# Summing a small matrix product on VectorE instead of TensorE, in one layer of a two-block transformer kernel

## The chip, the cores and the metric

The kernel runs on one core of a Trainium2 chip. Its time is the device time of one execution, in microseconds (us); before the change it is 1560.64 us, the median of three runs (1558.99 to 1562.67). The profile is one execution taken by the hardware profiler. TensorE is called PE in its rows (PEld is its weight load), VectorE is DVE, ScalarE is ACT, GpSimd is POOL, and SP is the queue that starts the transfers (DMAs).

## The reference, cut to what matters

The program is a transformer: a first block of two layers on 256 tokens `x` and 256 context tokens `ctx` with 1024 features, then a second block of two layers on `x` alone. All data is float32. Each of the first block's layers is modulated by vectors that depend on a conditioning vector `c`:

```python
s_lat, s_ctx = silu(c), silu(c_ctx)              # vectors of 1024
for i in range(2):
    mod   = s_lat @ w_mod[i] + b_mod[i]          # 1024 x 6144 weights; a vector of 6144
    mod_c = s_ctx @ w_mod[i] + b_mod[i]          # the same for the context tokens
    x, xc = _layer(x, xc, mod, mod_c, rope, i < 1, p)   # the last layer returns no context
# in _layer: six chunks of 1024 each
sh1, sc1, g1, sh2, sc2, g2 = split(mod, 6)       # csh1, csc1, ... from mod_c
h = rms_norm(x) * g_pre * (1 + sc1) + sh1        # hc from xc in the same way
...                                              # mixers on h and hc, x = x + g1 * norm(y)
h = rms_norm(x) * g_pre * (1 + sc2) + sh2        # the feed-forward part
x = x + g2 * norm(square(relu(h @ w_ff1)) @ w_ff2)
```

The second layer (i = 1) needs its context tokens only as keys, values and states, so of its `mod_c` only the chunks sh1 and sc1 are used.

## The kernel before

Tokens go in four tiles of 128 (x 0, x 1, ctx 0, ctx 1), features in K tiles of 128. Every large product is done by `mm3`: a float32 operand is split into a high part (rounded by ScalarE, line 226) and a low part (source minus high part, by VectorE, line 227), and three products high x high, high x low and low x high are summed in PSUM (line 212). Weights are fetched in transfers of 512 KB into the pool `raw` (five buffers of 128 x 1024) and split into the pools `wh` and `wl` (ten buffers of 128 x 512 each). A raw buffer is given back when both halves of it have been split.

The modulation of the second layer is computed inside the feed-forward part of the first layer, `ffn(0, ...)`. That has eight rounds (`r_` from 0 to 7). A round has a first half, in which w_ff1's block gives four outputs of 24 matmuls each (one per `ft`), and a second half, in which w_ff2's rows give eight outputs of 12 matmuls each. After each `ft` of the rounds 1 to 7 the code calls `step(1)`, 28 calls in all, which advances a generator: `mod_steps` (line 284). One step fetches one K tile of 2048 columns of w_mod in two transfers of 512 KB and issues four float32 matmuls with a stationary operand of 128 x 32 (two columns of it hold the vectors for x and ctx), one for each 32-partition band of one PSUM bank (`fl`, line 303). Eight steps make a unit; the ninth copies the bank (line 307), transposes it in four blocks (line 310) and adds the bias into `mods[1]` (line 314). Three units give the six chunks: 24 such steps with 96 matmuls.

In the first half ScalarE applies relu and square to each output (lines 902, 903), GpSimd squares it again in full precision (line 904) and VectorE subtracts to get the low part (line 905). In the second half VectorE adds each output to an accumulator (line 921).

The order on each engine is made by a scheduler: it takes instructions in the order of the program as their inputs and buffers come free in its own model of time. On the chip each engine then runs its list strictly in order. Buffers that matter here: `q` (eight of 128 x 512; four hold the gates of `ffn` until round 7), `fl` (one PSUM bank), and five PSUM banks `mm` and `sc` that the outputs use in turn.

Of the kernel before, what the change touches and what calls it, by code (L numbers as in the profile page):

```python
# [26 lines left out]
def constants():  # L27
# [4 lines left out]
    # positions of the 256 tokens ordered by (t mod 4, t // 4 mod 4, t // 16)  # L32
# [11 lines left out]
    # rope of the latent attention: 32 dims as four blocks of 8  # L44
# [7 lines left out]
    # rope of the second block: 64 dims as two halves  # L52
# [12 lines left out]
def body(ctx, tc, A, out):  # L65
# [49 lines left out]
    def AN():  # L115
        """A bank of either kind in turn."""
        turn[0] += 1
        return MM() if turn[0] % 3 == 1 else SC()
# [13 lines left out]
    def bc(ap, n):  # L132
        """[128, h] as [128, h, n]."""
        return ap[:, :, None].to_broadcast([ap.shape[0], ap.shape[1], n])

    def sooner(offset):
        """Scheduled ahead of the order of the program by an offset, later for a negative one."""
# [7 lines left out]
    def steps_sooner(offset):  # L145
        """The same for the steps of a generator."""
# [13 lines left out]
    # ---- pieces  # L160
# [3 lines left out]
    def rpow(out, a, b, eps):  # L164
        """(a + b + eps) ** -0.5"""
# [4 lines left out]
    def wblk(src, segs, k0=0, nk=KT, keep=0, tag="u"):  # L170
        """Weight rows of nk K tiles, columns `segs`, as pairs of high and low parts by K tile."""
# [35 lines left out]
    def mm3(ps, pairs):  # L207
        """Sum over the pairs of stationary^T @ moving, each as a high and a low part."""
# [9 lines left out]
    def tok(hT, t, W):  # L218
        """Pairs for token tile t against the weights of one block."""
        return [(cut(hT[k], t * P, (t + 1) * P), W[k]) for k in range(len(W))]  # L220
# [8 lines left out]
    def silu2(o, src):  # L229
        """2 silu(src) = src * (1 + tanh(src / 2))"""  # L230
# [7 lines left out]
    # ---- what every phase uses  # L238
# [8 lines left out]
    def load_cols(i, eng):  # L247
        """Vectors of layer i, feature on partition: [128, 110]."""
# [15 lines left out]
    # residual streams, token-major, as two halves of the features: ctx 0, ctx 1, x 0, x 1  # L264
# [8 lines left out]
    # ---- modulation  # L273
# [10 lines left out]
    def mod_steps(i, segs, w, ps):  # L284
        """Modulation of layer i: four segments of w columns, given by their starts; feature on partition."""
# [33 lines left out]

    def mod_units(*units):  # L320
        """A step function for the given (layer, pair of chunks) pairs, to be called between other work."""
# [3 lines left out]
        it = steps()  # L325
# [8 lines left out]
    def mod_scale(i, chunk, o_g, ks=(0, 8), a=None):  # L334
        """gain * (1 + scale)"""
# [7 lines left out]
    def mod_gate(i, chunk, o_g, r):  # L343
        """gate * gain of the norm after it, the same row on all partitions."""
# [14 lines left out]
    def normed(tiles):  # L359
        """RMS norm of token tiles, without a gain."""  # L360
# [12 lines left out]
    def modulated(xn, kind, scale, shift, dst, ks=range(KT), o=0):  # L373
        """Modulation and transposition of normed token tiles into the pairs dst[k] from column o on, [feature, token]."""
# [11 lines left out]
    def postnorm(t, halves, gate):  # L386
        """x[t] += gate * rms_norm(y)."""
# [8 lines left out]
    def softmax(ps, n):  # L396
        """Softmax of the rows of [128, n]."""
# [7 lines left out]
    def softmax_masked(ps, mask):  # L405
        """Softmax of the rows of mask - scores, given the scores with the sign turned; the mask is 0 or far above."""
# [7 lines left out]
    def transposed(p, nb, tag):  # L414
        """The nb blocks of p, each transposed, side by side in SBUF."""
# [7 lines left out]
    def interleaved(parts, order):  # L423
        """Interleaves generators by their letters, then ends each of them."""
# [6 lines left out]
    # ---- first block  # L431
    X, CTX = (2, 3), (0, 1)

    def both():
        """Pairs by K tile for ctx and x side by side, and their two parts."""
# [3 lines left out]
    def mix(i, hT, W1, step):  # L439
        """Both mixers of layer i up to w_out: the pairs of the concatenated outputs, [feature, token]."""  # L440
# [28 lines left out]
        # latent attention and dt: columns of one block  # L469
        # K tiles 0 to 3 of the concatenated outputs by feature, 4 to 7 by token tile  # L470
# [9 lines left out]
        def to_y(src, k, t, n, eng=None):  # L480
            """Columns of n tokens from tile t on, into pair k."""
# [22 lines left out]
        def latents():  # L504
            for t in X + CTX:
# [27 lines left out]
                # the two latents, transposed  # L533
# [5 lines left out]
                # keys and values  # L539
# [12 lines left out]
                # queries  # L552
# [25 lines left out]
        def attention():  # L578
            """CTX queries see the ctx keys, x queries all."""
# [744 lines left out]
```

## Time and profile before

| | |
|---|---|
| time of a run, median of 3 | 1560.64 us (1558.99 to 1562.67) |
| span of the profiled execution, first to last instruction | 1557.8 us |
| TensorE busy | 1490.3 us, 96% |
| VectorE busy | 951.7 us, 61% |
| ScalarE busy | 737.4 us, 47% |
| GpSimd busy | 298.2 us, 19% |
| TensorE's granted clock, mean | 0.985 |

The profile gives the span of its execution, and no separate time for it; the median of the runs is 2.84 us above this span. A busy share is an average over the whole span. What bounds one stage is read from the busy time of the engines in that stretch and from the waits before their instructions.

### The profile page before, as it was taken

How to read it: one execution, taken by the hardware profiler on the slowest of the kernel's cores; microseconds unless marked ns; L12 is line 12 of the kernel's file. 1: busy time of each engine (PE TensorE's matmuls, PEld its weight loads, DVE VectorE, ACT ScalarE, POOL GpSimd, SP SyncE). 2: the span in 40 equal slices, each digit the busy share in tenths (PEclk: the TensorE clock that was granted, in tenths of full speed). 3: DMA queues.
4: the chain of work that ended last, by engine and by line, in shares of the span. 5: the costliest groups of instructions: out<-in, count | busy, mean ns of one | idle time of the engine just before them, and what ended most of it. 6: DMA issues, size and time to landing. Idle time of an engine off the chain costs nothing.

```text
span 1557.8 us, 23537 instructions
## 1 busy us (share of the span) xinstructions
PE 1490.3 (96%) x8573; PEld 1217.5 (78%) x8573; DVE 951.7 (61%) x1919; ACT 737.4 (47%) x1589; POOL 298.2 (19%) x354
## 2 busy tenths in 40 slices
PE   6988999999999999997989899999999999999998
PEld 4756678887777777777977689997888888878886
DVE  3668555562444333457796765666785786567866
ACT  3433445553233322336555655555466457535653
POOL 1235201240000110024141201112310220021110
PEclk9998999999999999998999999999999999999999
DMA  9754623324555535534314555565535551545442
GB/s 301 251 199 151 197 95 102 97 67 129 173 172 176 188 105 180 185 94 121 98 61 130 163 160 179 168 227 163 167 118 163 163 188 35 199 153 169 144 149 68
DMA packets 123431, 235.47 MB, mean 151 GB/s; under 512 B 11536, under 2 KB 29139, under 8 KB 123315
## 3 DMA queue, kind: packets, MB, share of 16 engines
q1 hardware_dynamic: 122432, 232.42, 46.1%
q0 software_dynamic: 704, 1.50, 0.3%
q8 instruction: 67, 1.10, 0.3%
q14 instruction: 49, 0.40, 0.1%
q10 hardware_dynamic: 179, 0.06, 0.0%
HBM read 232.82 MB, written 1.11 MB: 150 GB/s over the span
## 4 chain that ended last, share of the span: by engine, by line
PE 83%; DVE 7%; DMA 5%; issue 2%; ACT 1%; POOL 1%; SPq 0%; ACTq 0%; DVEq 0%; POOLq 0%
PE sc L212 47%; PE mm L212 21%; PE fl L303 3%; PE tp L418 3%; DVE wl L227 2%; DMA raw<-in_w_mod_dram 1%; DMA raw<-in_ple_w_gate_dram 1%; DVE u L737 1%; PE mm L594 1%; PE sc L1038 1%; PE fl L212 1%; PE sc L748 1%; PE sc L1063 1%; PE sc L589 1%; PE tp L379 1%
## 5 line engine op out<-in xcount | busy, mean ns | idle before, releaser
L227 DVE TENSOR_TENSOR wl<-raw,wh 128x512 fp32r<-128x512 f32 (+1 forms) x602 | 418.1, 730 | 209.4 <-ACT wh L226 206.3
L226 ACT CAST wh<-raw 128x512 fp32r<-128x512 f32 (+1 forms) x602 | 355.8, 620 | 312.3 <-PE sc L212 74.1
L212 PE MATMUL sc<-wh,u 128*128 128x512 f32 (+2 forms) x1416 | 458.4, 391 | 2.2 <-ACT u L226 1.9
L212 PEld LDWEIGHTS sc<-wh,u 128*128 128x128 f32 x1416 | 264.8, 189 | 59.1 <-ACT wh L226 4.5
L212 PE MATMUL sc<-wl,u 128*128 128x512 f32 (+2 forms) x708 | 273.6, 388 | 0.1
L212 PE MATMUL sc<-u,wh 128*128 128x256 f32 (+1 forms) x1072 | 266.7, 337 | 1.6 <-ACT wh L226 1.0
L212 PE MATMUL mm<-wh,u 128*128 128x512 f32 (+1 forms) x648 | 218.9, 395 | 1.0 <-ACT u L226 1.0
L212 PEld LDWEIGHTS sc<-u,wh 128*128 128x128 f32 x1072 | 183.6, 191 | 31.3 <-issue 9.6
L212 PE MATMUL sc<-u,wl 128*128 128x256 f32 (+1 forms) x536 | 178.6, 335 | 0.0
L212 PEld LDWEIGHTS sc<-wl,u 128*128 128x128 f32 x708 | 134.2, 190 | 24.8 <-DVE wl L227 0.5
L904 POOL TENSOR_TENSOR r<-r 128x256 f32<-128x256 f32 (+1 forms) x60 | 57.7, 963 | 447.4 <-ACT r L902 404.2
L212 PEld LDWEIGHTS mm<-wh,u 128*128 128x128 f32 x648 | 122.0, 189 | 26.2 <-ACT u L226 1.7
L212 PE MATMUL mm<-wl,u 128*128 128x512 f32 (+1 forms) x324 | 126.7, 391 | 0.0
L212 PE MATMUL mm<-u,wh 128*128 128x256 f32 (+1 forms) x512 | 117.6, 317 | 0.1
L212 PEld LDWEIGHTS sc<-u,wl 128*128 128x128 f32 x536 | 102.1, 191 | 9.7
L905 DVE TENSOR_TENSOR u<-r,u 128x256 fp32r<-128x256 f32 (+1 forms) x60 | 33.7, 562 | 112.8 <-POOL r L904 110.2
L212 PEld LDWEIGHTS mm<-u,wh 128*128 128x128 f32 x512 | 85.8, 191 | 10.3 <-issue 4.2
L212 PE MATMUL mm<-u,wl 128*128 128x256 f32 (+1 forms) x256 | 80.7, 315 | 0.0
L971 POOL TENSOR_TENSOR r<-r,r 128x512 f32<-128x512 f32 (+1 forms) x30 | 44.7, 1493 | 151.1 <-DVE r L969 151.0
L212 PEld LDWEIGHTS mm<-wl,u 128*128 128x128 f32 x324 | 61.5, 190 | 11.9
L303 PE MATMUL fl<-raw,c_sT 128*32 128x512 f32 (+1 forms) x576 | 65.2, 475 | 4.5 <-DMA raw<-in_w_mod_dram 2.9
L902 ACT ACTIVATE r<-sc 128x256 f32<-128x256 f32 (+1 forms) x42 | 20.5, 489 | 97.1 <-PE sc L212 97.0
(308 smaller groups left out, 1947.5 us busy)
## 6 DMA issues: line engine op xcount, KB each, us to landing
raw<-in_w_ff_dram SPq DMA_DIRECT2D x128, 512.0 KB, 4.9
raw<-in_w_mod_dram SPq DMA_DIRECT2D x80, 512.0 KB, 4.5
raw<-in_a_w_in_dram SPq DMA_DIRECT2D x80, 512.0 KB, 3.7
raw<-in_w_in_dram SPq DMA_DIRECT2D x32, 512.0 KB, 3.9
raw<-in_b_w_in_dram SPq DMA_DIRECT2D x18, 512.0 KB, 4.8
raw<-in_w_mod_dram SPq DMA_DIRECT2D x32, 256.0 KB, 5.0
raw<-in_w_out_dram SPq DMA_DIRECT2D x16, 512.0 KB, 3.8
raw<-in_ple_w_gate_dram SPq DMA_DIRECT2D x16, 512.0 KB, 4.3
```

The costliest lines, as they stand in the source:

```text
L212: PE.matmul(ps, s, m, start=(i == 0), stop=(i == n - 1))
L226: ACT.copy(h, src)
L227: (eng or DVE).tensor_tensor(l, src, f(h), ALU.subtract)
L303: PE.matmul(ps[32 * g:32 * g + 32, :], sT[:, k + q, :], rs[g // per][:, q, w * (g % per):w * (g % per) + w], start=(k + q == 0), stop=(k + ...
L379: PE.transpose(tp[:, q * P:(q + 1) * P], xn[q][k // 4][:, (k % 4) * P:(k % 4 + 1) * P], ident)
L418: PE.transpose(tp[:, b * P:(b + 1) * P], p[:, b * P:(b + 1) * P], ident)
L589: PE.matmul(ps[:, b * P:(b + 1) * P], qT[t][:, hs], kT[b][:, hs], start=True, stop=True, skip_group_check=True)
L594: PE.matmul(po[64 * e:64 * e + 64, hp * P:(hp + 1) * P], V[b // 2][:, 256 * (b % 2) + 64 * h:256 * (b % 2) + 64 * h + 64], pT[e][:, b * P: ...
L902: ACT.activation(r[:, a:b], ps[:, a:b], AF.Relu)
L904: POOL.tensor_tensor(f2[:, a:b], r[:, a:b], r[:, a:b], ALU.mult)
L905: DVE.tensor_tensor(l, f2[:, a:b], f(h), ALU.subtract)
L971: POOL.tensor_tensor(a[:, 0:w], a[:, 0:w], b[:, 0:w], ALU.add)
```

## The change

The second layer's modulation is done by a new generator `mod_sums`. VectorE multiplies each half of a fetched tile (128 x 512 of one K tile) by the vector's entries, one scalar per partition, and adds the product to an accumulator of 128 x 512 in the pool `q`. After all eight K tiles the accumulator holds, per partition, the sum over row tiles; TensorE then sums over the partitions by a matmul with a stationary operand of ones (128 x 32). Four accumulators make one group: both vectors for the column blocks 0, 1, then both for 2, 3, then the vector for x alone for the blocks 4 to 7 and 8 to 11 (so the context vector is computed for the first two chunks only). Each transfer now holds two K tiles of 512 columns; there are 48 transfers of 512 KB, as before. `step(2)` is called in place of `step(1)`; the generator has 52 steps and there are 28 calls. The file also loses its comments and docstrings. Line numbers below the new code grow by 41 (905 becomes 946, 921 becomes 962).

```diff
+    ones = C([P, 32], "c_ones")
+    POOL.memset(ones, 1.0)
+
+    def mod_sums(i):
+        nrow = A["w_mod"][i].rearrange("(k p) n -> p k n", p=P)
+        for kinds, nb, b0 in (((0, 1), 2, 0), ((0, 1), 2, 2), ((0,), 4, 4), ((0,), 4, 8)):
+            accs = []
+            for b in range(b0, b0 + nb):
+                acc = [Q() for _ in kinds]
+                accs += acc
+                for k in range(0, KT, 2):
+                    r = raw.tile([P, 1024], F32, tag="raw", name=nm("raw")).rearrange("p (k c) -> p k c", k=2)
+                    SP.dma_start(r, nrow[:, k:k + 2, 512 * b:512 * b + 512])
+                    for q in range(2):
+                        for o, a in zip(kinds, acc):
+                            w = sT[:, k + q, o:o + 1]
+                            if k + q == 0:
+                                DVE.tensor_scalar(a, r[:, q, :], w, None, ALU.mult)
+                            else:
+                                DVE.scalar_tensor_tensor(a, r[:, q, :], w, a, ALU.mult, ALU.add)
+                    yield
+            ps = FL()
+            for g, a in enumerate(accs):
+                PE.matmul(ps[32 * g:32 * g + 32, :], ones, a, start=True, stop=True, skip_group_check=True)
+            r = R()
+            ACT.copy(r, ps)
+            for j in range(4):
+                PE.transpose(ps[:, j * P:(j + 1) * P], r[:, j * P:(j + 1) * P], ident)
+            ...
+            for b in range(nb):
+                k = 4 * (b0 + b)
+                DVE.tensor_tensor(mods[i][:, k:k + 4, 0:nr], t4[:, b, :, :, 0],
+                                  cols[i][:, O_BM + k:O_BM + k + 4, None].to_broadcast([P, 4, nr]), ALU.add)
+            yield
...
-                        step(1)
+                        step(2)
...
-    step = mod_units((1, 0), (1, 1), (1, 2))
+    POOL.memset(mods[1], 0.0)
+    step = stepping(mod_sums(1))
```

The scheduler moves instructions. On TensorE, after the first output of round 2 (24 matmuls; `wh`, `wl` are the weight's parts, `u` the activations', `fl` the modulation's bank) there stood before:

```order
L212 MATMUL sc989_4066<-u620_2608,wh979_4054 128x512
L212 MATMUL sc989_4066<-u621_2609,wh979_4054 128x512
L212 MATMUL sc989_4066<-u620_2608,wl980_4055 128x512
L303 MATMUL fl915_3740<-raw992_4097,c_sT8_114 32x512 x2
L303 MATMUL fl915_3740<-raw993_4099,c_sT8_114 32x512 x2
L212 MATMUL sc994_4105<-u606_2594,wh962_4020 128x512
```

At the same place there now stand the four matmuls that close the first group (`q` are accumulators):

```order
L212 MATMUL sc993_4088<-u621_2610,wh983_4076 128x512
L212 MATMUL sc993_4088<-u622_2611,wh983_4076 128x512
L212 MATMUL sc993_4088<-u621_2610,wl984_4077 128x512
L346 MATMUL fl996_4119<-q916_3743,c_ones13_124 32x512
L346 MATMUL fl996_4119<-q917_3744,c_ones13_124 32x512
L346 MATMUL fl996_4119<-q928_3831,c_ones13_124 32x512
L346 MATMUL fl996_4119<-q929_3832,c_ones13_124 32x512
L212 MATMUL sc1001_4140<-u607_2596,wh966_4042 128x512
```

They stand once in a group and not once in a K tile, so in the round there is no such insertion after the other three outputs. The second group's are not together: in the second half of round 2 TensorE's list has one of them alone.

```order
L212 MATMUL mm1042_4367<-wh1031_4297,u988_4083 128x512
L212 MATMUL mm1042_4367<-wh1034_4303,u989_4084 128x512
L346 MATMUL fl1078_4508<-q999_4133,c_ones13_124 32x512
L212 MATMUL mm1042_4367<-wl1035_4304,u989_4084 128x512
L212 MATMUL mm1042_4367<-wh1034_4303,u990_4085 128x512
```

In all they stand at seven places: four together, then one, one and two, then four together, then one and three. On VectorE, from the last accumulation of round 1 into round 2, there stood before the four low parts of round 2's outputs (line 905) and the weight's low parts (line 227) for its second half:

```order
L921 TENSOR_TENSOR u883_3659<-u883_3659,mm960_4004 128x512
L905 TENSOR_TENSOR u982_4059<-r991_4092,u981_4058 128x512
L905 TENSOR_TENSOR u984_4061<-r996_4131,u983_4060 128x512
L227 TENSOR_TENSOR wl1011_4225<-raw1009_4222,wh1010_4224 128x512
L227 TENSOR_TENSOR wl1013_4229<-raw1009_4222,wh1012_4228 128x512
L905 TENSOR_TENSOR u986_4063<-r1001_4170,u985_4062 128x512
```

Now the second group's products (lines 340 and 342) come first; the piece shows the first of them.

```order
L962 TENSOR_TENSOR u884_3662<-u884_3662,mm964_4026 128x512
L340 TENSOR_SCALAR q998_4132<-raw1000_4134,c_sT8_114 128x512
L340 TENSOR_SCALAR q999_4133<-raw1000_4134,c_sT8_114 128x512
L340 TENSOR_SCALAR q1010_4220<-raw1012_4222,c_sT8_114 128x512
L340 TENSOR_SCALAR q1011_4221<-raw1012_4222,c_sT8_114 128x512
L342 SCALAR_TENSOR_TENSOR q998_4132<-raw1000_4134,c_sT8_114,q998_4132 128x512
L342 SCALAR_TENSOR_TENSOR q999_4133<-raw1000_4134,c_sT8_114,q999_4133 128x512
L946 TENSOR_TENSOR u986_4081<-r995_4114,u985_4080 128x512
L342 SCALAR_TENSOR_TENSOR q1010_4220<-raw1012_4222,c_sT8_114,q1010_4220 128x512
```

Between the last accumulation of round 1 and the first low part of the weights for round 2's second half there are now 4 TENSOR_SCALAR and 18 SCALAR_TENSOR_TENSOR products; q998 takes the buffer of a first-group accumulator, which is free when the four matmuls above have run. Behind `ffn(0)` the lists of all engines are the same but for some swaps of neighbours.

## Rows read from the trace of the kernel before

**Rows 1.** The page: span, busy times, slices of TensorE and its clock.
```profile
span 1557.8 us, 23537 instructions
PE 1490.3 (96%) x8573; PEld 1217.5 (78%) x8573; DVE 951.7 (61%) x1919; ACT 737.4 (47%) x1589; POOL 298.2 (19%) x354
```

**Rows 2.** Windows of 40 us in ffn(0): busy by engine, clock, DMA share, GB/s.
```profile
400.00:440.00 40.00, 40.00 (x189) 29.37 (x188) 12.90 (x20) 10.21 (x18) 3.32 (x4) 1.00 0.45 144
...
sum 320.00, PE 319.95 PEld 243.18 DVE 122.94 ACT 97.10 POOL 29.50; mean PE 39.99 PEld 30.40 DVE 15.37 ACT 12.14 POOL 3.69
```

**Rows 3.** The tile fl from 300 to 690 us: count, duration min/median/max, forms.
```profile
L303 PE MATMUL fl<-raw,c_sT x192: 592/593/617, 368.7 to 664.4; 128*32 128x512 f32 x192
...
L314 DVE TENSOR_TENSOR c_mod<-fl,c_cols x6: 158/165/177, 472.6 to 677.9; 128x16 f32<-128x16 f32 x6
```

**Rows 4.** TensorE's timeline (start us, duration us): start of round 1; one step; one transposition.
```profile
363.20 0.39 PE L212 MATMUL sc<-u,wh 128*128 128x512 f32 x1
...
416.39 0.62 PE L212 MATMUL sc<-u,wh 128*128 128x512 f32 x2
416.84 0.39 PE L212 MATMUL sc<-u,wl 128*128 128x512 f32 x1
417.16 1.06 PE L303 MATMUL fl<-raw,c_sT 128*32 128x512 f32 x8
418.16 0.73 PE L212 MATMUL sc<-u,wh 128*128 128x512 f32 x2
...
471.62 0.39 PE L212 MATMUL mm<-u,wh 128*128 128x512 f32 x1
471.85 0.60 PE L310 MATMUL fl<-c_ident,r 128*128 128x128 f32 x4
472.20 0.48 PE L212 MATMUL mm<-u,wh 128*128 128x512 f32 x1
```

**Rows 5.** VectorE's groups from 360 to 690 us: count, busy us, mean ns.
```profile
L227 DVE TENSOR_TENSOR wl<-raw,wh 128x512 fp32r<-128x512 f32 (+1 forms) x108 | 73.6, 714 | 82.4 <-ACT wh L226 82.2
L921 DVE TENSOR_TENSOR u<-u,sc 128x512 f32<-128x512 f32 x33 | 22.6, 686 | 32.4 <-PE sc L212 32.1
L905 DVE TENSOR_TENSOR u<-r,u 128x512 fp32r<-128x512 f32 x28 | 19.3, 688 | 81.7 <-POOL r L904 81.7
```

**Rows 6.** VectorE, two lines of the whole program: duration min/median/max in ns.
```profile
L394 DVE SCALAR_TENSOR_TENSOR x<-r,s,x x16: 739/748/948, 293.0 to 1072.8; 128x512 f32<-128x512 f32 x16
L394 DVE SCALAR_TENSOR_TENSOR u<-r,s,u x8: 739/744/1210, 316.2 to 719.9; 128x512 f32<-128x512 f32 x8
...
L369 DVE TENSOR_SCALAR q<-x,s x16: 479/484/491, 7.5 to 888.6; 128x512 f32<-128x512 f32 x16
```

**Rows 7.** VectorE by shape, whole program: one more group with two tensors.
```profile
L1220 DVE SCALAR_TENSOR_TENSOR r<-r,u 128x512 f32<-128x512 f32 x8 | 5.4, 689 | 7.4 <-ACT r L1219 7.3
```

**Rows 8.** Timelines of VectorE and SP at the end of round 0.
```profile
345.63 0.42 DVE L905 TENSOR_TENSOR u<-r,u 128x256 fp32r<-128x256 f32 x1 [0.51 <-POOL r L904]
...
343.95 32.87 SPq L297 DMA_DIRECT2D raw<-in_w_mod_dram  x8
```

**Rows 9.** Transfers of w_mod: from issue to landing.
```profile
DMA to landing us min/median/max: 3.6/4.7/7.7
```

**Rows 10.** SP's waits from 360 to 690 us: total us, times, longest.
```profile
SPq L297 <- DVE wl L227: 97.6, 30, 8.6
SPq L297 <- PE fl L303: 71.3, 10, 17.7
```

**Rows 11.** All engines around 391 us, and line 904 from 360 to 690 us.
```profile
390.54 1.30 DVE L227 TENSOR_TENSOR wl<-raw,wh 128x512 fp32r<-128x512 f32 x2 [0.65 <-ACT wh L226]
...
391.65 1.08 POOL L904 TENSOR_TENSOR r<-r 128x512 f32<-128x512 f32 x1 [6.89 <-ACT r L902]
392.06 1.82 DVE L227 TENSOR_TENSOR wl<-raw,wh 128x512 fp32r<-128x512 f32 x2 [0.23 <-ACT wh L226]
...
L904 POOL TENSOR_TENSOR r<-r x28: 1039/1040/1132, 369.6 to 676.9; 128x512 f32<-128x512 f32 x28
```

More of the change, by code (lines that the diff above doesn't have):

```diff
@@ L318, in mod_steps @@
         yield
+    ones = C([P, 32], "c_ones")
[25 more added lines that the diff above has]
+                PE.transpose(ps[:, j * P:(j + 1) * P], r[:, j * P:(j + 1) * P], ident)
+            nr = len(kinds)
+            t4 = ps.rearrange("p (j b r q) -> p b j r q", j=4, b=nb, r=nr)
+            for b in range(nb):
[3 more added lines that the diff above has]
+            yield
     def mod_units(*units):
@@ L324, in steps, with stepping @@
                 yield from mod_steps(i, [2048 * u + 512 * g for g in range(4)], 512, FL())
-        it = steps()
+        return stepping(steps())
+    def stepping(it):
         def step(n=1):
```

## The prediction

> **What bounds the kernel now.** I read the page first, then the windows of the stretch that the change touches, then the tile of the modulation's bank, then timelines of single places. The page shows TensorE busy for 96% of a span of 1557.8 us, VectorE for 61% [rows 1]. The windows from 360 to 680 us, rounds 1 to 7 of `ffn(0)`, are what counts: TensorE is busy for 319.95 of 320 us at a granted clock of 1.00 in each window, VectorE for 122.94 us [rows 2]. Time taken from TensorE there is time saved, as long as VectorE, which has some 197 us free there on average, delivers its parts in time. The tile of the bank gives what can be taken: 192 passes of line 303 (each of the 96 matmuls is two passes), all inside these rounds [rows 3].
>
> **TensorE, what goes.** An undisturbed matmul follows the one before it by 0.226 us: two in the 0.45 us from 416.39 to 416.84. Across one step of the modulation it is 418.16 - 416.84 = 1.32 us [rows 4]. A step costs 1.32 - 0.23 = 1.09 us, and 24 of them 26.2 us.
>
> **TensorE, what comes.** Sixteen summing matmuls have the form of the old ones (128 x 32 stationary, 512 columns). Four together I take at the price of a step, 1.09 us. The order has them at seven places, some alone; no row shows one alone. Two passes cannot cost more than eight, so 1.09 us a place is the upper end, 7.6 us for seven; the lower end is 16/96 of the old cost, 4.4 us. I take 7.6, since entering and leaving the narrow form is visible beside the passes (0.32 us from 416.84 to 417.16 instead of 0.23). The fourth group adds one set of four transposes: 472.20 - 471.62 - 0.23 = 0.35 us [rows 4]. TensorE thus loses 26.2 - 7.6 - 0.35 = 18.2 us of work; with the lower end 21.5.
>
> The Trainium skill bears on the lone ones: its page "TensorEngine Tiling (Array Packing)", section Tiling Modes, says that a change of the tiling mode drains TensorE. By that rule every place would pay the drain whatever it holds, which is the upper end, the value taken.
>
> **VectorE, what comes.** 128 products of 128 x 512: 16 that start an accumulator and 112 that add to one. For the first kind there is a row, 484 ns; for the second the nearest is line 394, also two tensors and a scalar per partition, 748 ns [rows 6]. The ends are 689 ns, from a row whose scalar is a constant [rows 7], and 1210 ns, the longest of line 394 [rows 6]. I take 748, the median of the same form: 16 x 0.484 + 112 x 0.748 = 91.5 us. The bias additions become twelve instead of six, 1 us more at 165 ns [rows 3]. Averaged over the rounds this fits. It isn't spread evenly: the first two groups take 64 products, for which rounds 1 and 2 have about 44 us each. VectorE's old work in a round is 16 low parts of weights, 8 accumulations and 4 low parts of outputs at about 0.69 us [rows 5], 19 us; 32 products add 4 x 0.484 + 28 x 0.748 = 22.9. That is 42 of 44 us, so in these two rounds the order within the queue decides.
>
> Round 1. The products can start once the first transfer has landed: issued at 343.95 [rows 8], 4.7 us to land [rows 9], so 348.7; VectorE's last task of round 0 ends at 346.05 [rows 8]. In the new order 18 products of 748 ns, 4 of 484 ns and 6 low parts of weights stand up to the last low part for the round's first output: 19.5 us, until 368.2. TensorE starts the round at 363.20 [rows 4] and needs this part after 29 matmuls, at 369.8. It fits with 1.6 us to spare. I put 1 us for waits here.
>
> Round 2. The second group needs the accumulators of the first, which are free once the four summing matmuls behind the round's first output have run, 24 x 0.226 + 1.09 = 6.5 us into the round. Then 4 + 18 products, two low parts of outputs, two bias additions and the first low part of a weight: 1.9 + 13.5 + 1.4 + 0.3 + 0.7 = 17.8, ready at 24.3 us. TensorE wants it after 96 matmuls, one place, one set of transposes and three more matmuls, at 23.9 us: 0.4 us late. Behind it products and low parts alternate at the pace at which they are wanted. Near the round's end the low parts for round 3 wait in VectorE's queue for their transfers, whose raw buffers come free only when the products are done (up to now TensorE freed them), and the accumulations of line 962, which free the PSUM banks, stand behind: by the same reckoning about 2 us.
>
> GpSimd adds to this. Where line 904 ran for 1.08 us at 391.65, the pair of low parts beside it took 1.82 us instead of 1.30 [rows 11]: 0.5 us lost for one. Up to three fall into the busy stretch of round 2: 1.6 us. Waits in round 2 come to 4 us.
>
> Rounds 3 to 7. With 16 products of 11 to 12 us a round VectorE is at 31 of 44 us. Its waits for an accumulator's buffer fall in the first half of a round, ahead of work that is wanted in the second. I put nothing; the cover is VectorE's 12 us of free time a round.
>
> **Transfers.** 48 of 512 KB before and after. SP has waited 97.6 us for low parts and 71.3 us for line 303 to free a raw buffer [rows 10]; the second kind now waits for VectorE. DMA is busy for 0.45 of the time in the window shown [rows 2], so I see no new bound there. The two memsets are GpSimd's, which is busy for 19% [rows 1].
>
> **Sum.** -18.2 + 1 + 4 = -13.2 us, a span of 1544.6. The profile gives no time of its own execution beyond its span; the median of the runs is 2.84 us above it. Keeping that, 1547.4, so **1547.5 us**, 0.8% faster. A difference below 0.2% (3.1 us) can't be told from none.
>
> **Rivals.**
>
> *GpSimd and VectorE shut each other out.* The row at 391.65 shows half a microsecond lost for one line 904. If each of them stops a full VectorE queue for its whole 1.04 us [rows 11], rounds 1 and 2 lose 8 x 1.04 = 8.3 us beside the 2.4 us of round 2: 18.2 - 10.7 = 7.5 us gained, 1553.1 us. Against it: VectorE lost half of 1.04, and round 1 has 1.6 us to spare. Chance 0.12. The Trainium skill, page "SBUF — State Buffer", section SBUF: two separate sides, has the rule: a VectorE operation with two SBUF inputs and a GpSimd operation that reads SBUF hold the shared port pair exclusively, for a whole instruction. The trace agrees with a loss and not with its full length.
>
> *VectorE becomes the bound in rounds 1 and 2, no change.* With products at 0.98 us, halfway to 1.21, the 56 adding products of these rounds take 13 us more, all of it behind a queue that is already full: -13.2 + 13 = 0, about 1560.5 us. For it: 42 of 44 us. Against it: in both groups of line 394 the median lies within 9 ns of the minimum, so 1210 was an exception. Chance 0.11. At 1.21 us each it would be 26 us and 1573, which I leave outside.
>
> *The raw buffers starve the weights, slower.* Five buffers serve products and weights. A tile whose four products take 3 us is held longer than by a 1.09 us step, and a weight's transfer is issued behind it. Every round has two weight blocks, 14 in all. If the last transfer of each comes late by half a landing, 2.35 us, TensorE loses 33 us against 18.2: 14.7 us slower, 1575 us. The point from which it decides is 18.2 / 14 = 1.3 us a block. For it: the 71.3 us SP already waits for line 303. Against it: in five of the seven rounds a tile has only two products of 1.5 us in all, and DMA is under half busy. Chance 0.09.
>
> That the change doesn't do what it says, leaving products for the end, I exclude: 28 calls of two steps cover 52 steps.
>
> **How the numbers follow.** The forecast with waits between 0 and 10 us, 1542 to 1552: 0.62. More than 18.2 us, since lone matmuls are cheaper: 0.06. Then 0.12, 0.11 and 0.09 as above. Faster: 0.62 + 0.06 + 0.12 = 0.80; same 0.11; slower 0.09. The range of 1541 to 1559 leaves out some 0.03 below, three quarters of the case without change and the slower one, 0.2 in all.
>
> **What would show it.** Line 303 has no passes behind 360 us; lines 346 and 350 take about 8 and 2 us. Rounds 3 to 7 get shorter by 3 to 4 us each, round 2 hardly. VectorE is busy some 92 us more. In round 2 TensorE waits for wl of line 227 and for line 962, about 4 us; if it waits more than 10 us there, or waits for wh and transfers in rounds 3 to 7, I am wrong. Line 342 far from 748 ns makes the second rival right. Behind 700 us nothing changes but the start.

## The result, and the profile after

The changed kernel takes 1545.02 us, the median of four runs (1543.72 to 1545.77), beside 1561.14 us (1558.99 to 1562.67) for the kernel before, which has a fourth run by now: ratio 0.9895, 95% interval 0.9883 to 0.9907. Run once more, in a series of its own, it took 1542.54 us (1538.66 to 1545.70) beside 1559.97: 0.9882, interval 0.9862 to 0.9901. It is faster, by 16.1 and 17.4 us; forecast were 1547.5 us and 13 us. Single runs of one kernel scatter, and the longer ones mostly show a lower granted clock: of the six runs of that series the shortest, 1538.66 us, had 0.988 and the longest, 1545.70 us, 0.981.

The page, as in [rows 1]: TensorE has lost 16 us of work, VectorE has gained 85.

```profile
span 1544.0 us, 23412 instructions
...
PE 1474.4 (95%) x8417; PEld 1216.4 (79%) x8417; DVE 1036.5 (67%) x2053; ACT 740.0 (48%) x1590; POOL 307.3 (20%) x356
```

The windows of [rows 2] (busy us of PE, PEld, DVE, ACT, POOL, with instruction counts; clock; DMA share; GB/s). TensorE is no longer quite full, from 440 to 480 us above all; VectorE goes from 122.94 to 213.37 us.

```profile
400.00:440.00 40.00, 39.87 (x181) 31.76 (x180) 28.73 (x44) 10.38 (x18) 5.66 (x4) 1.00 0.39 118
440.00:480.00 40.00, 39.04 (x166) 29.21 (x165) 29.59 (x49) 11.81 (x21) 3.87 (x3) 1.00 0.70 224
480.00:520.00 40.00, 40.00 (x178) 33.13 (x177) 27.55 (x44) 12.12 (x21) 3.72 (x3) 1.00 0.65 210
...
sum 320.00, PE 318.90 PEld 256.92 DVE 213.37 ACT 106.84 POOL 43.34; mean PE 39.86 PEld 32.11 DVE 26.67 ACT 13.36 POOL 5.42
```

The tile of the bank, as in [rows 3]: 32 passes in place of 192. The last row tells who waited for the bank: twice the first product of a group (line 340) could not start before the sums of the group ahead had freed its accumulator, 9.6 us of VectorE's time in all.

```profile
L346 PE MATMUL fl<-q,c_ones x32: 592/605/617, 416.0 to 649.9; 128*32 128x512 f32 x32
...
L350 PE MATMUL fl<-c_ident,r x16: 270/272/276, 422.3 to 657.0; 128*128 128x128 f32 x16
...
  DVE q L340: 9.6, 2
```

Where the time went is read from the first matmul of each round (start, duration). The kernel before, profiled a second time (the starts of rounds 1, 2 and 7):

```profile
364.71 0.61 PE L212 MATMUL sc<-u,wh 128*128 128x512 f32 x2
...
413.14 0.62 PE L212 MATMUL sc<-u,wh 128*128 128x512 f32 x2
...
653.35 0.62 PE L212 MATMUL sc<-u,wh 128*128 128x512 f32 x2
```

The changed kernel, rounds 1 to 7:

```profile
366.92 0.62 PE L212 MATMUL sc<-u,wh 128*128 128x512 f32 x2
...
410.44 0.62 PE L212 MATMUL sc<-u,wh 128*128 128x512 f32 x2
...
459.75 0.62 PE L212 MATMUL sc<-u,wh 128*128 128x512 f32 x2
...
504.95 0.39 PE L212 MATMUL sc<-u,wh 128*128 128x512 f32 x1
...
548.47 0.61 PE L212 MATMUL sc<-u,wh 128*128 128x512 f32 x2
...
594.91 0.62 PE L212 MATMUL sc<-u,wh 128*128 128x512 f32 x2
...
638.43 0.62 PE L212 MATMUL sc<-u,wh 128*128 128x512 f32 x2
```

Rounds 1 to 6, from the first row to the last, take 288.64 us before (288.57 in the first profile) and 271.51 after: 17.1 us less, which is the result. One by one the rounds after take 43.52, 49.31, 45.20, 43.52, 46.44 and 43.52; before, a round with four steps takes 48.43. Rounds 1, 4 and 6 have no matmul of the modulation any more, so **43.52 us is the bare round**. That gives the price of each place at which matmuls of the modulation stand, from whole rounds:

- a step, eight passes in one place: (48.43 - 43.52) / 4 = 1.23 us;
- round 3 has one place of passes and one set of transposes: 45.20 - 43.52 = 1.68, so a set of four transposes costs 0.45 us;
- round 5 has in addition a place with two passes alone: 46.44 - 45.20 = 1.24 us;
- round 2 has three places and one set, 3 x 1.23 + 0.45 = 4.14, but is 5.79 us above the bare round: 1.65 us are waits;
- before the change, rounds 3 and 5 took 47.51 and 47.35 us. Each had a step, a set, and one place where two steps stood side by side, so these sixteen passes cost 2.31 and 2.15 us.

The first of these two places, in TensorE's timeline of the kernel before:

```profile
477.18 1.93 PE L303 MATMUL fl<-raw,c_sT 128*32 128x512 f32 x16
```

Sixteen passes are busy for 1.93 us, eight for 1.06 and two for 1.05 (rows below), though each pass takes 0.6 us. So the matmuls of the four bands run beside each other, and a place costs the same only up to one matmul for each band; a second one behind it costs about 1 us more.

In the experiments below, places and sets in rounds 1 to 6 are counted in the timeline, and "rest" is what remains of the six rounds above 6 x 43.52 + 1.23 a place + 0.45 a set: waits of TensorE. (Before the change the 22 are steps, at 20 places. The rest is below zero there, since a pair of steps side by side is a little cheaper than two apart.)

| kernel | rounds 1 to 6, us | places, sets | rest, us | median of runs, us | ratio to before (95%) |
|---|---|---|---|---|---|
| before | 288.57 | 22, 2 | -0.5 | 1561.14 | |
| changed | 271.51 | 6, 3 | 1.7 | 1545.02 | 0.9895 (0.9883, 0.9907) |
| the same again | 271.52 | 6, 3 | 1.7 | 1542.54 | 0.9882 (0.9862, 0.9901) |
| products thin | 266.25 | 3, 3 | 0.1 | 1541.33 | 0.9877 (0.9862, 0.9892) |
| products twice | 282.10 | 10, 3 | 7.3 | 1552.03 | 0.9951 (0.9934, 0.9968) |
| both vectors for all | 277.09 | 9, 5 | 2.7 | 1550.05 | 0.9939 (0.9922, 0.9955) |
| two chunks on TensorE | 274.33 | 10, 2 | 0.0 | 1545.38 | 0.9913 (0.9898, 0.9928) |
| sums together | 267.87 | 3, 3 | 1.7 | 1540.42 | 0.9867 (0.9842, 0.9891) |
| products spread | 268.73 | 5, 3 | 0.1 | 1543.11 | 0.9882 (0.9861, 0.9904) |
| no square on GpSimd | 270.25 | 6, 3 | 0.4 | 1545.07 | 0.9889 (0.9864, 0.9913) |
| together and spread | 267.34 | 3, 3 | 1.2 | 1540.18 | 0.9867 (0.9844, 0.9890) |
| the same again | 268.38 | 3, 3 | 2.2 | 1542.37 | 0.9881 (0.9858, 0.9904) |
| sums apart | 281.52 | 14, 3 | 1.8 | 1552.40 | 0.9966 (0.9951, 0.9981) |

The median less the six rounds lies between 1269.9 and 1275.1 us in every row: the rounds explain the times, to some 2.5 us of scatter. All but three kernels have a single profile, and the rest is not the same in each execution: the two profiles of "together and spread" have 1.2 and 2.2 us of it.

### The profile page after: what moved, and what is told of

The parts are those of the page before. It is cut to its first block, busy times and chain, and to the rows that moved or that the text cites. A ratio compares the mean times of both kernels' runs of the same rounds, so it can differ in the third digit from the quotient of the medians.

```text
span 1544.0 us, 23412 instructions
## 1 busy us (share of the span) xinstructions
PE 1474.4 (95%) x8417; PEld 1216.4 (79%) x8417; DVE 1036.5 (67%) x2053; ACT 740.0 (48%) x1590; POOL 307.3 (20%) x356
## 4 chain that ended last, share of the span: by engine, by line
PE 81%; DVE 9%; DMA 5%; issue 2%; ACT 2%; POOL 1%; SPq 0%; ACTq 0%; DVEq 0%; POOLq 0%
PE sc L212 46%; PE mm L212 19%; PE tp L459 3%; DVE wl L227 2%; PE fl L303 2%; DMA raw<-in_w_mod_dram 2%; DMA raw<-in_ple_w_gate_dram 1%; DVE u L778 1%; PE mm L635 1%; PE sc L1079 1%; PE fl L212 1%; PE sc L789 1%; PE sc L630 1%; DMA raw<-in_w_in_dram 1%; PE sc L1104 1%
## 5 line engine op out<-in xcount | busy, mean ns | idle before, releaser
L945 POOL TENSOR_TENSOR r<-r 128x256 f32<-128x256 f32 (+1 forms) x60 | 64.1, 1069 | 421.6 <-ACT r L943 374.7
L342 DVE SCALAR_TENSOR_TENSOR q<-raw,c_sT,q 128x512 f32<-128x512 f32 x112 | 84.9, 788 | 14.1 <-DMA raw<-in_w_mod_dram 13.5
L227 POOL TENSOR_TENSOR u<-r,u 128x256 fp32r<-128x256 f32 (+1 forms) x48 | 38.9, 817 | 122.8 <-ACT u L226 122.6
```

The costliest lines, as they stand in the source:

```text
L227: (eng or DVE).tensor_tensor(l, src, f(h), ALU.subtract)
L342: DVE.scalar_tensor_tensor(a, r[:, q, :], w, a, ALU.mult, ALU.add)
L945: POOL.tensor_tensor(f2[:, a:b], r[:, a:b], r[:, a:b], ALU.mult)
```

## The experiments

The theory: in these rounds TensorE has next to no other waits, and the time is a bare round plus a fixed price for each place at which the narrow form (128 x 32) interrupts the large matmuls, with two passes as with eight. The rivals: VectorE, whose work has grown, sets part of the time; or the price goes by passes.

**Is VectorE's added work in the way? Thin products.** The products that add read and write 16 of 512 columns, so the modulation is left incomplete.

```diff
-                                DVE.scalar_tensor_tensor(a, r[:, q, :], w, a, ALU.mult, ALU.add)
+                                DVE.scalar_tensor_tensor(a[:, 0:16], r[:, q, 0:16], w, a[:, 0:16], ALU.mult, ALU.add)
```

> Each of the 112 adding products works on 16 columns instead of 512, so the modulation is not complete; transfers, buffers and summing matmuls stay, and the order now has the sums at four places instead of seven. My theory (the change is paid and earned in TensorE's own list, and VectorE's load costs TensorE only the 2 us of waiting in round 2): three places of 1.05 us and 2.2 us of waiting go, 5.4 us less than the changed kernel's 1545.0, so 1539.6. Rival (VectorE's load slows TensorE in every round, so that the gain could have been much larger): 8 us less or more, below 1537. Rival (TensorE waits for the raw buffers' transfers, not for VectorE): as the changed kernel but for the three places, 1542.

Measured 1541.33 us. A product took 238 ns in the mean instead of 788, some 62 us less for VectorE, and the six rounds lost 5.26 us. Of these, three places fewer make 3.7 us (each group's four sums now stand together), and the waits make 1.6. By its time alone the kernel stands nearer to the 1542 us of the rival with the raw buffers than to the theory's 1539.6. The rounds decide: by that rival only the three places would have gone, and the waits of round 2 are gone too. So VectorE's work costs next to nothing as such; it costs places and the waits of round 2.

**Products twice.** Each adding product is issued a second time, so the sums are other ones.

```diff
                                 DVE.scalar_tensor_tensor(a, r[:, q, :], w, a, ALU.mult, ALU.add)
+                                DVE.scalar_tensor_tensor(a, r[:, q, :], w, a, ALU.mult, ALU.add)
```

> Every adding product is issued twice, so the modulation's values change; VectorE has 112 x 0.75 = 84 us more. My theory (VectorE is hidden only as long as a round's work fits beside TensorE's 44 us): rounds 1 and 2 have 63 us of VectorE's work, of which some 17 us can be done in round 0, rounds 3 to 7 have 42 us; the time grows by 20 to 35 us to 1565 to 1580, nearly all of it in rounds 1 and 2. Rival (the raw buffers are what is short): every round grows by more than 3 us. Rival (VectorE has room enough everywhere): under 1550.

Measured 1552.03 us: this expectation was wrong, by far for the theory and by 2 us for the rival of room enough. VectorE is now all but full in the windows from 400 to 480 us, and 278.80 us busy in all:

```profile
400.00:440.00 40.00, 37.43 (x155) 27.26 (x154) 39.81 (x63) 8.94 (x15) 5.60 (x4) 0.99 0.40 127
440.00:480.00 40.00, 39.89 (x162) 30.31 (x161) 38.93 (x62) 9.22 (x16) 1.50 (x2) 0.97 0.60 184
...
sum 320.00, PE 316.21 PEld 249.22 DVE 278.80 ACT 100.15 POOL 44.64; mean PE 39.53 PEld 31.15 DVE 34.85 ACT 12.52 POOL 5.58
```

Yet 112 more products, 87.7 us of work, cost 10.6 us in the rounds: 5 are places (ten instead of six, since sums that come later fall apart) and 5.6 waits, with a dip of the granted clock to 0.97 within them. The longest wait is for a high part of a weight; another is for a low part (in brackets the idle time before the matmul and what ended it):

```profile
436.85 0.50 PE L212 MATMUL sc<-wh,u 128*128 128x512 f32 x1 [1.45 <-ACT wh L226]
...
439.01 0.50 PE L212 MATMUL sc<-wl,u 128*128 128x512 f32 x1 [0.65 <-DVE wl L227]
```

I had held the products of a group to the rounds in which the kernel calls them. They are not held there: of the 120 products of the first two groups 18 ran in round 0, 42 and 51 in rounds 1 and 2, and 9 in round 3. VectorE took them up in rounds that it filled almost to the end: 44.32 of 46.20 us in round 1 and 52.69 of 52.87 us in round 2.

**The price of a place: sums apart.** Each accumulator is summed as soon as it is complete, so that the same 16 matmuls stand at 15 places.

```diff
-            accs = []
+            ps, todo, g = FL(), [], 0
...
+                    if k == KT - 2:
+                        todo += acc
+                    if todo:
+                        PE.matmul(ps[32 * g:32 * g + 32, :], ones, todo.pop(0), start=True, stop=True, skip_group_check=True)
+                        g += 1
                     yield
...
-            for g, a in enumerate(accs):
+            for a in todo:
...
```

> Each accumulator is summed over its partitions as soon as it is complete, not when its group is: the same 16 summing matmuls now stand at 15 places, 14 of them in rounds 1 to 6, where the changed kernel has 6. Theory (a place costs about 1.2 us, whatever it holds): rounds 1 to 6 take 6 x 43.54 + 14 x 1.2 + 3 x 0.48 = 279.5 us without waits, 8 us more than the 271.5 of the changed kernel, 1553 us. Rival (the price goes by passes, 1.22 / 8 = 0.15 us each): 30 passes cost 4.6 us wherever they stand, rounds 1 to 6 take 267 us and as much as now beside the waits, 1541 to 1545 us.

Measured 1552.40 us, and 281.52 us for the six rounds. The rows are the start of round 1, a lone place, the only marked wait of the six rounds, and the start of round 7:

```profile
364.45 0.62 PE L212 MATMUL sc<-u,wh 128*128 128x512 f32 x2
...
375.42 1.04 PE L345 MATMUL fl<-q,c_ones 128*32 128x512 f32 x2
...
604.87 0.50 PE L212 MATMUL sc<-u,wl 128*128 128x512 f32 x1 [1.77 <-DVE wl L227]
...
645.97 0.62 PE L212 MATMUL sc<-u,wh 128*128 128x512 f32 x2
```

281.52 - 1.77 = 279.75, against 279.5 by the theory and 267 by passes. Eight places more, with the same 32 passes in all (30 instead of 26 of them in these rounds), took 10.0 of the 17.1 us away. The rival is out: a count of all passes does not give the price. The theory holds as long as a place has at most one matmul in each band; with the sixteen passes above it does not.

**Sums together.** GpSimd makes the ones from the group's last accumulator (times 0, plus 1), so that none of the four sums can run before that accumulator is complete.

```diff
+            one = S(32)
+            POOL.tensor_scalar(one, accs[-1][:, 0:32], 0.0, 1.0, ALU.mult, ALU.add)
...
-                PE.matmul(ps[32 * g:32 * g + 32, :], ones, a, start=True, stop=True, skip_group_check=True)
+                PE.matmul(ps[32 * g:32 * g + 32, :], one, a, start=True, stop=True, skip_group_check=True)
```

> The operand of ones of each group is made from the group's last accumulator, so that the four summing matmuls come free together: four places instead of seven. From the rounds of the traces so far a place costs TensorE 1.2 us and not 1.09 (round 1 before: 48.43 us, 192 matmuls of 0.2266 us and four steps). My theory: three places less, 3.6 us less than the changed kernel, 1541.4; rounds 1 to 6 take 269.1 us (271.5 in the changed kernel; one of the three places is in round 5, two in round 2). Rival (the lone matmuls fill time in which TensorE waits for VectorE anyway, which is why the scheduler put them there): the rounds 271.5, time as the changed kernel.

Measured 1540.42 us; the rounds take 267.87, 3.6 us less than in the changed kernel, for three places fewer (3.7). The 269.1 us that I had set down counted two of the three places; 271.5 less the 3.6 of the same sentence is 267.9.

**Products spread.** The calls advance the generator by one, two or three steps instead of always two, fewer in the first fourteen calls, more in the others.

```diff
+    plan = ([1, 1, 1, 2, 1, 1, 2] * 2) + [2, 3] * 6 + [2, 2]
...
-                        step(2)
+                        step(plan.pop(0) if i == 0 else 1)
```

> The steps are spread so that each call brings four to six products: 18 steps in the first 14 calls, 34 in the last 14. The sums stand at six places, five of them in rounds 1 to 6. My theory (the 1.6 us that TensorE waits in round 2 come from 32 products in one round): no waits, rounds 1 to 6 in 261.2 + 5 x 1.2 + 3 x 0.48 = 268.7 us, time 2.8 us below the changed kernel, 1542.2. Rival (the wait comes from the changeover of accumulators and comes with any order): one place less, 270.3 us, 1543.8.

Measured 1543.11 us, rounds 268.73: the 1.6 us of waits are gone, and a place too. Its round 1 holds one lone place and nothing else of the modulation:

```profile
365.71 0.62 PE L212 MATMUL sc<-u,wh 128*128 128x512 f32 x2
...
401.16 1.04 PE L346 MATMUL fl<-q,c_ones 128*32 128x512 f32 x2
402.13 0.50 PE L212 MATMUL sc<-wh,u 128*128 128x512 f32 x1
...
410.43 0.62 PE L212 MATMUL sc<-u,wh 128*128 128x512 f32 x2
```

410.43 - 365.71 - 43.52 = 1.20 us for two passes alone.

**Where do round 2's waits come from? No square on GpSimd.** GpSimd's full-precision square is left out in rounds 1 to 7; the low part of the activations is taken from values without it.

```diff
-                    POOL.tensor_tensor(f2[:, a:b], r[:, a:b], r[:, a:b], ALU.mult)
+                    if i or not r_:
+                        POOL.tensor_tensor(f2[:, a:b], r[:, a:b], r[:, a:b], ALU.mult)
+                    else:
+                        f2 = r
```

> GpSimd's square is left out in rounds 1 to 7 (the low part of the outputs is computed from the value and not from its square), so GpSimd takes nothing from VectorE there. My theory: VectorE's products fall from a mean of 788 to 750 ns, and TensorE gains at most the 1.6 us it waits in round 2: rounds 1 to 6 in 270 to 271.5 us, 1543.5 to 1545. Rival (the shared port costs TensorE more than is seen as waiting): 5 us less or more, under 1540.

Measured 1545.07 us, which shows nothing of 1.3 us; the profile does. The products of the changed kernel (count, minimum/median/maximum in ns):

```profile
L342 DVE SCALAR_TENSOR_TENSOR q<-raw,c_sT,q x112: 736/747/1532, 354.0 to 630.3; 128x512 f32<-128x512 f32 x112
```

And without the square:

```profile
L342 DVE SCALAR_TENSOR_TENSOR q<-raw,c_sT,q x112: 737/745/753, 352.2 to 625.2; 128x512 f32<-128x512 f32 x112
```

TensorE's timeline without the square, the starts of rounds 2 and 3:

```profile
408.76 0.61 PE L212 MATMUL sc<-u,wh 128*128 128x512 f32 x2
...
456.41 0.62 PE L212 MATMUL sc<-u,wh 128*128 128x512 f32 x2
```

No product is held up any more, and round 2 takes 47.65 us instead of 49.31: its three places and its set, and no wait. (The second profile of the changed kernel has 49.04 us here.) The experiment also takes away the low part's wait for GpSimd, so it doesn't say how much of the 1.66 us is the one or the other.

**What is "context vector for two chunks" worth? Both vectors for all six chunks**, 192 products.

```diff
-        for kinds, nb, b0 in (((0, 1), 2, 0), ((0, 1), 2, 2), ((0,), 4, 4), ((0,), 4, 8)):
+        for kinds, nb, b0 in [((0, 1), 2, b) for b in range(0, 12, 2)]:
```

> Both vectors for all six chunks: 192 products in six groups, so VectorE has 42 us of work in nearly every round; sums at ten places and six sets of transposes. My theory: 3 x 1.05 + 2 x 0.35 = 3.9 us more on TensorE, and a wait of about 2 us as in round 2 in four more rounds, 8 us: 1557. Rival (the wait in round 2 is the changeover between groups alone, and a round of 42 us fits): 1549. Rival (VectorE can't be filled to 95% for long: the lag adds up from round to round): 1565 or more.

Measured 1550.05 us, 5 us above the changed kernel. The rounds are 5.6 us longer: three places (3.7), two sets (0.9), 1.0 of waits. The theory's 1557 us, with waits in four more rounds, were wrong, and the first rival's 1549 nearer; 64 products more are not what costs.

**Two chunks on TensorE.** The first two chunks by the old steps, the others by the new generator.

```diff
-        for kinds, nb, b0 in (((0, 1), 2, 0), ((0, 1), 2, 2), ((0,), 4, 4), ((0,), 4, 8)):
+        for kinds, nb, b0 in (((0,), 4, 4), ((0,), 4, 8)):
...
-                        step(2)
+                        step(plan.pop(0) if i == 0 else 1)
...
+    def parts():
+        yield from mod_steps(1, [512 * g for g in range(4)], 512, FL())
+        yield from mod_sums(1)
+
+    plan = [1] * 9 + [2] * 15 + [1] * 4
-    step = stepping(mod_sums(1))
+    step = stepping(parts())
```

> The first two chunks, which need both vectors, go the old way on TensorE (eight steps), the other four by products on VectorE (64 products). My theory by TensorE's list: eight steps of 1.09 us come back, the four places of the first two groups (4.2 us), one set of transposes (0.35) and the wait in round 2 (2.2) go: 2 us more than the changed kernel, 1547. Rival (the full rounds 1 and 2 cost more than is seen as a wait): below 1544.

Measured 1545.38 us; rounds 274.33, eight steps and two places and no wait. Eight steps in place of the two context groups cost 2.8 us in the rounds and can't be told from the changed kernel in the time.

**Together and spread**: the edits of "sums together" and "products spread" at once.

> Both of the edits that may save something: steps spread evenly, and the four sums of a group together. My theory: three places of 1.2 us and 1.6 us of waiting less than the changed kernel, 5.2 us, 1539.8; rounds 1 to 6 in 261.2 + 3 x 1.2 + 3 x 0.48 = 266.2 us. Rival (accumulators that are given back together, and later, make VectorE wait, and TensorE with it): the rounds 269 us or more, 1542 or more.

Measured 1540.18 us. The rounds take 267.34 us, between what the two theories gave: no more than three places, but 1.2 us of waits. To settle whether this beats the changed kernel, both were run once more side by side:

> Sums together and products spread, beside the changed kernel. The rounds give 267.3 against 271.5 us, so 4.2 us under the changed kernel, 1541 us. If the earlier 4.8 us between their medians came from the chips, the two lie within 2 us of each other here.

> The changed kernel once more, on the same chip as the variant with the sums together and the products spread. By the rounds it should repeat: rounds 1 to 6 take 271.5 us, about 1545 us, 0.990 of the time before. If the first measurement lay low by scatter, the ratio comes nearer to 0.992, which is what the profiled execution (3.7 us late at round 1) showed.

1542.37 and 1542.54 us: **not told apart**. In the profiles the variant's six rounds are shorter in both pairs, by 4.2 and 3.1 us, and from the start of round 1 to the end of the span it is shorter by 4.0 and 2.7 us. The sums of the changed kernel's six rounds agree to 0.01 us, but by chance: round 2 is 0.27 us shorter and round 6 0.28 us longer the second time. Single runs of one kernel scattered by 7 to 11 us here, and 3 us vanish in that. It is the better version by its profiles, and not shown to be so by its time.

**Before, once more.**

> The kernel before, unchanged, with one more profile. In its profile round 1 began at 363.20 us, in those of the changed kernel and its variants at 364.4 to 370.2 us, though nothing was moved ahead of that point. If this is scatter of the arrival of the first transfers, round 1 begins here at 364 us or later, and rounds 1 to 6 take 288.6 us again. If the change delays the start in some way that the order doesn't show, round 1 begins at 363.2 us again.

Round 1 began at 364.71 us, the rounds took 288.64. So the start scatters without any change, if less than between 363.20 and 366.92; over all profiles of changed kernels it lay between 364.37 and 370.21. The products are not what makes it late: "two chunks on TensorE" has none before 451 us and began round 1 at 365.91. Whether a microsecond or two of that belongs to the change is open; the medians show no such loss.

## Why the prediction was right, step by step

**The mechanism and the sign held**: TensorE bounds these rounds, and what was taken from it came back as time.

**The price of a step was too small.** I took 1.09 us, from the row before a step's passes to the first matmul behind them [rows 4]. That stops too early. In the changed kernel (TensorE's timeline; a place with eight passes):

```profile
415.65 0.39 PE L212 MATMUL sc<-u,wl 128*128 128x512 f32 x1
415.97 1.06 PE L346 MATMUL fl<-q,c_ones 128*32 128x512 f32 x8
416.97 0.73 PE L212 MATMUL sc<-u,wh 128*128 128x512 f32 x2
417.54 0.39 PE L212 MATMUL sc<-u,wl 128*128 128x512 f32 x1
```

The two large matmuls behind the passes take 0.57 us from start to start, not 0.45. From 415.65 to 417.54 it is 1.89 us where three undisturbed matmuls take 0.68: 1.21, and 1.23 by whole rounds. A set costs 0.45 us and not 0.35. Rounds 1 to 7 had 30.4 us of steps and sets before (27.5 in rounds 1 to 6, 2.9 in round 7) and have 10.4 after (7 places, 4 sets): TensorE saves 20.0 us, not 18.2.

**A lone place costs as much as a full one**, as assumed. Two passes alone:

```profile
585.32 0.39 PE L212 MATMUL mm<-wh,u 128*128 128x512 f32 x1
585.64 1.05 PE L346 MATMUL fl<-q,c_ones 128*32 128x512 f32 x2
586.62 0.50 PE L212 MATMUL sc<-wh,u 128*128 128x512 f32 x1
586.95 0.39 PE L212 MATMUL sc<-wl,u 128*128 128x512 f32 x1
```

1.05 us busy for two, 1.06 for eight. The lower end, by passes, is refuted by the sums apart. But the reason that I gave, entering and leaving the narrow form, is the smaller part. Of the 1.21 us above, 1.00 lie between the first pass (415.97) and the next large matmul (416.97); 0.09 are lost ahead of it and 0.12 behind. The lone place costs as much because the passes of the four bands run beside each other, so that two need as long as eight; sixteen cost 2.15 to 2.31 us. The Trainium skill says that a change of the tiling mode drains TensorE ("TensorEngine Tiling (Array Packing)", Tiling Modes). The trace leaves room for that in the 0.2 us beside the passes, and no run here separates a drain from the rest.

**The waits were put too high**: 5 us against 1.7. Round 1 has none; I gave it 1. The reckoning that rounds 1 and 2 hold 64 products failed for round 1: 19 of the 128 products ran in round 0, 13 in round 1 and 34 in round 2. VectorE by rounds (the part of round 0 from 345.13; rounds 1 and 2; round 4):

```profile
345.13:366.92 21.79, 21.79 (x98) 18.03 (x97) 17.75 (x31) 10.40 (x20) 1.59 (x1) 1.00 0.66 213
366.92:410.44 43.52, 43.52 (x193) 36.05 (x192) 29.55 (x43) 14.61 (x25) 5.56 (x4) 1.00 0.50 159
410.44:459.75 49.31, 48.22 (x210) 36.48 (x208) 40.91 (x64) 14.58 (x25) 5.66 (x4) 1.00 0.54 165
...
504.95:548.47 43.52, 43.52 (x194) 36.05 (x192) 24.15 (x38) 14.10 (x24) 4.76 (x4) 1.00 0.50 163
```

VectorE's products began in round 0, as soon as the first transfer had landed (353.18, and not 348.7), and round 1 had 14 us to spare. Round 2 held about as much work for VectorE as predicted, 40.91 us, and its two waits stood where I put them, on line 227 and line 962. The first is for the first low part of a weight (timeline of all engines):

```profile
434.34 0.39 PE L212 MATMUL sc<-wh,u 128*128 128x512 f32 x1
434.86 0.19 PEld L212 LDWEIGHTS sc<-wl,u 128*128 128x128 f32 x1 [0.56 <-DVE wl L227]
434.86 0.50 PE L212 MATMUL sc<-wl,u 128*128 128x512 f32 x1
```

It comes 0.30 us late, 0.41 with the next matmul; 0.4 were predicted. In the second a weight lands late, ScalarE rounds it late (449.44), its low part waits for that (450.09), and behind it the accumulation that frees a PSUM bank comes late:

```profile
449.44 1.14 ACT L226 CAST wh<-raw 128x512 fp32r<-128x512 f32 x2 [2.81 <-DMA raw<-in_w_ff_dram]
450.09 0.69 DVE L227 TENSOR_TENSOR wl<-raw,wh 128x512 fp32r<-128x512 f32 x1 [2.66 <-ACT wh L226]
450.70 0.68 DVE L962 TENSOR_TENSOR u<-u,sc 128x512 f32<-128x512 f32 x1
...
451.44 0.50 PE L212 MATMUL sc<-wh,u 128*128 128x512 f32 x1 [0.96 <-DVE u L962]
```

That costs 1.23 us with the next matmul; about 2 were predicted. So the terms that were too high are the 1 us for round 1 (none came), the 2 us for the end of round 2 (1.23), and the 1.6 us for GpSimd, for which no wait of its own shows. Rounds 3 to 6 have none, as predicted: above the bare round only places and sets.

**Rounds.** "Rounds 3 to 7 shorter by 3 to 4 us each, round 2 hardly": rounds 3 to 6 are shorter by 2.3, 4.9, 0.9 and 4.9, so only the mean, 3.25, is as predicted; round 2 is 0.9 longer, and round 1, which I had not named, 4.9 shorter. "Behind 700 us nothing changes but the start": from the start of round 7 to the end of the span it is 906.0 and 905.6 us.

**VectorE.** Lines 340 and 342 took 93.4 us busy (8.5 + 84.9), 91.5 forecast; the median product was 747 ns, 748 taken from line 394, and the mean 788. On the page VectorE is busy for 84.8 us more, where "some 92" were forecast.

**The rivals.** *GpSimd and VectorE shut each other out*: there, and small. The square's absence takes every long product away, and with the low part's wait for GpSimd 1.3 us of the rounds; 8.3 were the price of this rival. The longest product took 1532 ns, 785 more than the median and three quarters of a square's 1042, so the half that I saw in [rows 11] is not the most; but only six products were long. Their delay is 4.7 us in all, of which 2.2 fell into round 2: three products, as reckoned, at 0.78 us instead of 0.5. Two of them stand ahead of the first wait of round 2, so they may have a part in it. The Trainium skill's rule that the two engines exclude each other from a shared port ("SBUF — State Buffer", SBUF: two separate sides) agrees with the trace: the longest product takes 1532 ns with the square and 753 ns without. *VectorE as the bound*: not at this load; even twice the products, which fill VectorE in round 2, cost only 5.6 us of waits more. *Raw buffers starve the weights*: there, and small. SP's weight transfers (line 180) and those of w_mod (line 335) wait 87.9 us for products in these rows, where 71.3 us went to line 303 [rows 10]:

```profile
SPq L180 <- DVE q L342: 54.2, 29, 13.6
SPq L335 <- DVE q L342: 33.7, 17, 9.6
```

Yet of TensorE's waits only the second of round 2 goes back to a weight that landed late: 1.23 us, where this rival had 33.

**The sum.** -13.2 us was forecast; rounds 1 to 7 give 20.0 - 1.7 = 18.3 us. Not all of it arrives: round 7 saves 1.2 us of this, but from its start to the end of the span the kernel is only 0.4 us shorter in the first pair of profiles and 0.0 in the second. So 17.1 to 17.5 us remain, and the runs say 16.1 and 17.4. The first profiled execution shows 13.8 (1557.8 to 1544.0), because it reached round 1 3.7 us later, which the medians don't bear out. Of the 2.84 us that I kept around the span, 1.8 are what lies around it (1545.77 - 1544.0 in the profiled run); the rest would be a profiled execution some 1 us shorter than the median run.

The step (1.8 us) and the waits (3.3 us) were both wrong in the same direction: put right, they would have made the forecast 1542.4 us. That 1547.5 came within 2.5 us of 1545.02 is in part luck, since round 7's saving did not arrive and the runs scatter; the second series, 1542.54, is 5 us below the forecast.

## What to carry to other kernels

Where TensorE is the bound, count the places at which small matmuls interrupt the large ones, not their passes, as long as a place has one matmul for each of the four bands: these run beside each other. Take the price of a place from whole rounds, since the matmuls behind the interruption are slower too. Here work moved to an engine with room cost little even where it filled that engine for a round; look for the few in-order neighbours that free PSUM banks or buffers. When a profile resolves microseconds that runs don't (7 to 11 us of scatter here), state the gain from the rounds and say that the time doesn't show it.

## What the runs showed of the hardware that I had not expected

Two passes of the 128 x 32 form between large matmuls cost 1.20 to 1.24 us, as much as eight in four bands, and 0.12 us of it falls on the two large matmuls behind; sixteen cost 2.15 to 2.31 us. The same order of instructions reached round 1 at 363.20 and 364.71 us in two profiles of the kernel before, and repeated its six rounds to 0.1 us. Where TensorE waits the rounds repeat less well: to 1.0 us in "together and spread". As far as these pairs go, most of the scatter of the runs, 7 to 11 us, arises outside these rounds.
